# A hybrid attention and convolution layer on one core: norm rows, rotary tables and cached keys loaded by SyncE behind the first modulation's weights, and ten idle products fewer at the start

## The chip, the core and the metric

The kernel runs on one core of a Trainium2 chip, in one launch. The metric is the device time of an execution in microseconds (us); lower is better. Of the engines, PE is TensorE (matmuls; its weight loads are listed apart as PEld), DVE is VectorE, ACT is ScalarE, POOL is GpSimd and SP is SyncE, which here only issues DMA transfers. A transfer can be issued by SP, ACT or POOL.

## What is computed

One layer of a diffusion backbone for 128 context tokens and 512 latent tokens (model width 1024). The reference, cut to what matters:

```python
mod = (silu(cond) @ w_ada + b_ada)                   # shift, scale, gate, twice
h = rms(x, norm_mix) * (1 + sc1) + sh1
q, k, v, gb, gc, u = split(h @ w_in)
q, k = rms(q, q_norm), rms(k, k_norm)                # per head of 64
attn = softmax(rope(q) @ [cache_k, rope(k)].T / 8) @ [cache_v, v]    # latent tokens
y_conv = gb * conv3(gc * u)
x = x + g1 * (concat(rms(attn), rms(y_conv)) @ w_out)
h2 = rms(x, norm_ffn) * (1 + sc2) + sh2
x = x + g2 * ((silu(gate) * up) @ w_down)            # gate, up = split(h2 @ w_gate_up)
```

Context tokens attend to context tokens alone and have no rotary positions. Outputs are the new x of both kinds of token and the context's new keys and values. The cache holds 128 keys and values; `rope` is a table of cosines and sines that is passed in.

## The kernel before, in words

Everything is float32; a product with full precision is made of three matmuls (`mm3`, lines 178 to 181) of a rounded high part and a low part of each operand. Weights come from memory in tiles of 512 KB (128 x 1024), ACT rounds them to a high part `wh`, DVE subtracts to get the low part `wl`.

The change lies in the first stage, some 60 us long, which makes the modulated input h and the query projection. Its steps are written out by hand:

- `P1SEQ` (line 33) is the order of the steps. The recorder goes through it once and each step puts its instructions on its engines, and on PE, DVE, ACT and POOL they stay in that order. The steps that matter here: `dN` is N idle products of the identity with itself (`spin`, line 502, one matmul each, which appears as two records in the trace); `rT` squares token tile T on ACT (line 445), `iT` adds up parts of the square on DVE (459), `kT` sums it on PE (466) and takes the power -1/2 on POOL (189), `oT` spreads it over a row (471, 472). `aK` multiplies the conditioning with the K-th part of the modulation's weights on PE (`ada1_mm`, line 383, sixteen matmuls in two halves of eight, one for each load); `bK` copies the result out, `mK` turns and adds it (427, 429) and makes the scale and shift `modA` and `modB` (399, 400). `gKT`, `hK` and `fKT`, `nK` make the high and low part of h (480, 481, 484), `qKT` is the query projection. `yI`, `zI` split the two halves of the first query weight (531, 535), `w`, `l` split the later weights (522, 539). `p0` is `rows2_load` (lines 544 to 551), `R` builds the rotary tables on DVE (560).
- `LOADS` (line 113) is the order in which SP issues the transfers of this stage: `x` a tile of tokens, `A` the two loads (`af`, 512 KB each) of the next part of the modulation's weights, `Q` and `V` the halves of the first query weight, `W` the next weight of the plan (the query weights 1 to 3, then two for keys and values, then convolution), `C` the cached keys and values (`y`, 64 KB each).

SP works through this list in order, and each issue waits until its buffer is free: there are four `af` buffers, so that the loads of `a2` are issued when PE has done `a0`, and so on, and three buffers (`wf`) for the other weights. Behind a waiting issue all others wait.

`rows2_load` stands in `P1SEQ` between the fourth and fifth part of the modulation. There POOL issues three loads: the norm rows of queries and of keys (64 numbers each, sent to all 128 partitions, 32 KB written) and the rotary tables (256 KB); then it makes four small copies that swap the halves of the norm rows. The rows and tables are read for the first time by step `R`. The cached keys are copied by ACT and the values are split at the start of the attention part, which follows; its instructions are ordered by a scheduler.

Of the kernel before, what the change touches and what calls it, by code (L numbers as in the profile page):

```python
# [15 lines left out]
P = 128  # L16
D = 1024
KD = D // P
NL = 4
# [3 lines left out]
HD = 64  # L23
# [6 lines left out]
NKEY = 640  # L30
EPS = 1e-6
CG = 32
P1SEQ = ('d20 r0 i0h d1 r1 i1e v0 d3 k0 d3 k1 d2 r2 d1 i2e r3 d1 i3f d1 o0 y0 k2 a0 b0 o1 k3 z0 d2 m0 o2 d2 o3 d1 g00 '
# [76 lines left out]
AHEAD = 3  # L110
OSQ = 2
AFB = 4
LOADS = 'xxxxAQAxVAAWCAAAWAWWWWW'
O_Q, O_K, O_GB, O_GC, O_U = 0, 512, 768, 1280, 1792


def build(ctx, tc, x_tiles, cond, cache_k, cache_v, vectors, b_ada, q_norm, k_norm, w_mod, w_ada,
          w_q, w_kv, w_conv, w_out, w_gate_up, w_down, rope, x_turned, o_turned, o_k, o_v):
    nc = tc.nc
    act, dve, pool, pe, sp = nc.scalar, nc.vector, nc.gpsimd, nc.tensor, nc.sync  # L120
# [23 lines left out]
    def T(tag, shape, dt=F32, bufs=1):  # L144
        seq[0] += 1
        return pools[where.get(tag, "A")][1].tile(list(shape), dt, tag=tag, bufs=bufs, name=f"{tag}_{seq[0]}")
# [46 lines left out]
    g = tc.tile_pool(name="R", bufs=1, space=bass.MemoryType.DRAM)  # L193
# [59 lines left out]
    def load_next(later=False):  # L253
        load(order[stream_at[0]], later)
        stream_at[0] += 1
# [81 lines left out]
    def x_load():  # L337
        t = next(xs)
        sp.dma_start(xT[:, t], x_tiles[t])

    def ada1_next(n):
        for _ in range(n):
            next(loads, None)
# [4 lines left out]
                                            mybir.EngineType.SP})  # L348
    pre_order.__enter__()
    first = []  # L350
    for a in LOADS:
        if a == "A":
            ada1_next(3)
        elif a == "W":
            load_next(True)
        elif a == "Q":
            first.append(T("wf", (P, 2, 512), F32, WFB))
            sp.dma_start(first[0][:, 0], order[0][1][:, 0])
            stream_at[0] += 1
        elif a == "V":  # L360
            sp.dma_start(first[0][:, 1], order[0][1][:, 1])
        elif a == "C":
            cc = T("y", (P, 2, NKV, HD))
            ck, cv = cc[:, 0], cc[:, 1]
            sp.dma_start(ck, cache_k[0, 0])
            sp.dma_start(cv, cache_v[0, 0])
        else:
            x_load()
# [18 lines left out]
    def vec_do():  # L387
        for i, (bo, no) in enumerate(((8, V_MIX), (32, V_FFN))):
            dve.scalar_tensor_tensor(nb[:, i], vec[:, bo:bo + KD], 1.0, vec[:, no:no + KD], ALU.add, ALU.mult)
# [148 lines left out]
        wf, wh, wl = rounded.pop(0)  # L538
        eng.tensor_tensor(wl, wf, f32(wh), ALU.subtract)

    gain_rows = {nm: T("gn" + nm, (P, 2, HD)) for nm in "qk"}
    rt = T("oz", (P, 2, NL, HD))

    def rows2_load():
        for nm, g in (("q", q_norm), ("k", k_norm)):
            pool.dma_start(gain_rows[nm][:, 0], g[0].partition_broadcast(P))
        pool.dma_start(rt, rope)
        for nm in "qk":
            g0, g1 = (gain_rows[nm][:, i].rearrange("p (a b c) -> p a b c", a=2, b=2) for i in range(2))
            for b in range(2):  # L550
                pool.tensor_copy(g1[:, :, b], g0[:, :, 1 - b])
# [15 lines left out]
    def q_evict(t):  # L567
# [3 lines left out]
        else:  # L571
            act.activation(qraw[t], qps[t], AF.Copy)

    steps = {"r": x_square, "k": x_rms, "o": x_row, "y": first_hi, "c": late_consts, "w": w_hi, "p": lambda i: rows2_load(),
             "v": lambda i: vec_do(), "m": ada1_mod, "a": ada1_mm, "d": spin, "E": q_evict,
             "R": lambda i: rope_tables(),
             "X": lambda i: act.activation(warm, warm, AF.Exp)}
# [2 lines left out]
    in_pre[0] = True  # L580
    for x in P1SEQ.split():
        k = int(x[1:] if x[0] == "d" else x.strip("p")[1:2] or 0)
# [70 lines left out]
    def k_turn(kd, kt):  # L653
        tag = KTAG[kt]
        tp = PS2()[:, 0, :NKV * P].rearrange("p (v q) -> p v q", v=NKV) if tag == "s" else PB((P, NKV, P), tag=tag)
        for v in range(NKV):
            pe.transpose(tp[:, v], kd[:, v].rearrange("p a d -> p (a d)"), ident)
        ks = slice(kt * P, (kt + 1) * P)
        split(KA[:, :, ks], KB[:, :, ks], tp)
# [4 lines left out]
    def kv_mm(t):  # L664
        acc = PB((P, 256), tag="c")
        s = slice(t * P, (t + 1) * P)
        for k in range(KD):
            wh, wl = W(("kv", k // 4))
            mm3(acc, hH[k][:, s], hL[k][:, s], wh[:, k % 4], wl[:, k % 4], k == 0, k == KD - 1)
        kd = head_norm(acc[:, 0:P], NKV, t, 1)  # L670
        vt = T("vt", (P, NKV, HD), F32, 2)
        act.activation(vt, acc[:, P:].rearrange("p (h d) -> p h d", d=HD), AF.Copy)
        v_store(vt, 0 if t == CTX else t + 2)
        if t == CTX:
            sp.dma_start(o_k[0, 0], kd[:, :, 0])
            sp.dma_start(o_v[0, 0], vt)
        return kd

    def q_split(t):
        return head_norm(qraw[t], NH, t, 0)  # L680

    def q_turn(st, t):
        q = T("qT", (P, NH, P), F32R, QTB)
        tp = PB((P, 4, P)) if t not in QS else PS2()[:, 0].rearrange("p (g q) -> p g q", g=4)
        for g in range(4):
            pe.transpose(tp[:, g], st[:, 2 * g:2 * g + 2].rearrange("p a d -> p (a d)"), ident)
        pairs = q.rearrange("p (g a) q -> p g a q", a=2)
        top, low = slice(0, HD), slice(HD, P)
        with early(QTP):
            for a, x, y in ((0, top, low), (1, low, top)):  # L690
                act.activation(pairs[x, :, a], tp[x], AF.Copy)
                dve.tensor_tensor(pairs[y, :, a], tp[x], f32(pairs[x, :, a]), ALU.subtract)
        return q
# [326 lines left out]
    def k_first():  # L1020
        ks["c"] = k_twice(1)
        act.activation(ks["c"], ck.unsqueeze(2).to_broadcast([P, NKV, 2, HD]), AF.Copy)
        v_store(cv, 1)

    def rms_of(t):
        if t == CTX or t >= 0:
            att_rms(t)

    steps = {"k": lambda t: ks.update({t: kv_mm(t)}), "K": lambda t: k_turn(ks.pop(t), 0 if t == CTX else t + 2),
             "q": lambda t: qs.update({t: q_split(t)}), "Q": lambda t: qT.__setitem__(t, q_turn(qs.pop(t), t)),  # L1030
             "F": F, "A": lambda i: next(ada_gen, None), "c": lambda t: k_first(), "C": lambda t: k_turn(ks.pop("c"), 1),
             "a": ctx_s, "t": ctx_t, "o": ctx_o, "r": att_rms, "M": mix_att}
    for x in SEQ.split():
        if "." in x:
            n, i = (int(y) for y in x[1:].split("."))
# [105 lines left out]
    r2, r2p = {}, {}  # L1141
# [361 lines left out]


tile_hymba = with_exitstack(build)

_INS = ["x_tiles", "cond", "cache_k", "cache_v", "vectors", "b_ada", "q_norm", "k_norm", "w_mod", "w_ada",
# [70 lines left out]
```

## Time and profile before

| | us |
|---|---|
| median of 3 runs | 718.66 (714.97, 718.66, 719.32) |
| the profiled execution | 715.23 |
| its span | 713.5 |
| PE busy | 704.2 |
| DVE busy | 547.4 |
| ACT busy | 418.6 |
| POOL busy | 66.6 |

The span runs from the first to the last instruction of the profiled execution; the rest of its 715.23 us lies around it. A row of the profile's timeline gives the start and the length in us, the engine, the line of the code, what is written and read, how many records, and in brackets how long the engine stood idle before and what ended that. A row of the DMA issues gives what is moved, the engine that issues, how many times, KB of one, and the median of us from the issue to the landing. A row of the stretches gives for each engine the us that it was busy in the stretch and the number of records that start in it, then the granted clock of TensorE, the mean busy share of the 16 DMA engines, and GB/s.

### The profile page before, as it was taken

To read this page: it belongs to the slowest core of one execution; us is meant where nothing else is said; L and a number is where in the kernel's file an instruction comes from. 1 tells how busy PE (TensorE), PEld (TensorE's weight loads), DVE (VectorE), ACT (ScalarE), POOL (GpSimd) and SP (SyncE) were. 2 spreads that over 40 slices of the span, in tenths; PEclk is the share of its full clock that TensorE was granted. 3 is DMA by queue.
4 is the path that set the end of the run, shared out by engine and by line. 5 is a ranking of instruction groups with operands and counts; after the bars stand their busy time and mean duration, and the time that the engine had idled before them with its cause. 6 is when DMAs were issued, how large, how long until landed. Compare 5 with 4: busy or idle time off the path is not lost.

```text
span 713.5 us, 12614 instructions
## 1 busy us (share of the span) xinstructions
PE 704.2 (99%) x4935; PEld 677.7 (95%) x4935; DVE 547.4 (77%) x994; ACT 418.6 (59%) x798; POOL 66.6 (9%) x95
## 2 busy tenths in 40 slices
PE   9899999999999999999999999999999999999998
PEld 8579879988999999999999999999999999999997
DVE  4789979776777746789898966679889756788895
ACT  5456767766677535666565655455556545465553
POOL 2203111112010221300000011000000011000000
PEclk9999999999999999999999999999999999999999
DMA  9957385246322223811222257512222566312462
GB/s 344 342 215 257 119 300 209 72 157 159 154 57 74 61 80 92 278 65 60 90 89 90 89 131 154 127 60 93 85 89 89 126 135 134 110 60 83 140 214 97
DMA packets 34027, 95.95 MB, mean 134 GB/s; under 512 B 4304, under 2 KB 12624, under 8 KB 31920
## 3 DMA queue, kind: packets, MB, share of 16 engines
q1 hardware_dynamic: 29504, 88.09, 35.9%
q0 software_dynamic: 4176, 7.01, 6.9%
q8 instruction: 38, 0.62, 0.3%
q14 instruction: 21, 0.17, 0.1%
q10 hardware_dynamic: 288, 0.05, 0.0%
HBM read 81.77 MB, written 10.62 MB: 129 GB/s over the span
## 4 chain that ended last, share of the span: by engine, by line
PE 96%; DMA 2%; ACT 1%; DVE 0%; issue 0%; POOL 0%; DVEq 0%; POOLq 0%
PE pf L179 22%; PE pf L180 22%; PE pf L181 22%; PE pc L711 4%; PE pc L712 4%; PE pc L713 4%; PE ps L837 2%; PE po L881 2%; PE pt L864 2%; PE pc L768 2%; PE pc L502 2%; DMA af<-in_w_mod_dram 1%; PE ps L179 1%; PE pc L383 1%; PE ps L181 1%; PE ps L180 1%
## 5 line engine op out<-in xcount | busy, mean ns | idle before, releaser
L1348 DVE TENSOR_TENSOR wl<-sx,wh 128x1024 fp32r<-128x1024 f32 (+1 forms) x64 | 75.9, 1186 | 45.9 <-ACT wh L1345 45.9
L179 PE MATMUL pf<-B,wh 128*128 128x320 f32 x288 | 89.1, 309 | 0.0
L180 PE MATMUL pf<-B,wh 128*128 128x320 f32 x288 | 88.9, 309 | 0.0
L181 PE MATMUL pf<-B,wl 128*128 128x320 f32 x288 | 88.9, 309 | 0.0
L181 PE MATMUL pf<-T,wl 128*128 128x320 f32 x280 | 86.6, 309 | 0.0
L180 PE MATMUL pf<-T,wh 128*128 128x320 f32 x280 | 86.5, 309 | 0.0
L179 PE MATMUL pf<-T,wh 128*128 128x320 f32 x280 | 86.5, 309 | 0.0
L1345 ACT ACTIVATE wh<-sx 128x1024 fp32r<-128x1024 f32 (+1 forms) x64 | 65.7, 1027 | 3.8 <-PE pf L180 3.3
L711 PE MATMUL pc<-hH,wh 128*128 128x320 f32 x192 | 61.2, 319 | 0.0
L713 PE MATMUL pc<-hH,wl 128*128 128x320 f32 x192 | 59.3, 309 | 0.0
L712 PE MATMUL pc<-hL,wh 128*128 128x320 f32 x192 | 59.3, 309 | 0.0
L180 PEld LDWEIGHTS pf<-B,wh 128*128 128x128 f32 x288 | 54.1, 188 | 0.0
L179 PEld LDWEIGHTS pf<-B,wh 128*128 128x128 f32 x288 | 54.1, 188 | 0.0
L181 PEld LDWEIGHTS pf<-B,wl 128*128 128x128 f32 x288 | 54.1, 188 | 0.0
L181 PEld LDWEIGHTS pf<-T,wl 128*128 128x128 f32 x280 | 52.6, 188 | 0.1
L179 PEld LDWEIGHTS pf<-T,wh 128*128 128x128 f32 x280 | 52.6, 188 | 0.0
L180 PEld LDWEIGHTS pf<-T,wh 128*128 128x128 f32 x280 | 52.6, 188 | 0.0
L180 PE MATMUL pf<-gT,wh 128*128 128x320 f32 x160 | 49.4, 308 | 0.0
L179 PE MATMUL pf<-gT,wh 128*128 128x320 f32 x160 | 49.4, 308 | 0.0
L181 PE MATMUL pf<-gT,wl 128*128 128x320 f32 x160 | 49.4, 308 | 0.0
L1345 ACT ACTIVATE wh<-wf 128x1024 fp32r<-128x1024 f32 (+3 forms) x48 | 42.6, 887 | 0.8 <-PE pf L180 0.8
L1348 DVE TENSOR_TENSOR wl<-wf,wh 128x1024 fp32r<-128x1024 f32 (+1 forms) x32 | 38.0, 1186 | 4.1 <-ACT wh L1345 4.1
(351 smaller groups left out, 1994.7 us busy)
## 6 DMA issues: line engine op xcount, KB each, us to landing
wf<-in_w_gate_up_dram SPq DMA_DIRECT2D x44, 512.0 KB, 3.3
aw<-in_w_ada_dram SPq DMA_DIRECT2D x10, 1024.0 KB, 5.7
af<-in_w_mod_dram SPq DMA_DIRECT2D x16, 512.0 KB, 7.2
wf<-in_w_down_dram SPq DMA_DIRECT2D x16, 512.0 KB, 3.5
wf<-in_w_conv_dram SPq DMA_DIRECT2D x12, 512.0 KB, 4.2
xd<-cu POOLq DMA_DIRECT2D x16, 320.0 KB, 4.3
mA<-in_w_ada_dram SPq DMA_DIRECT2D x4, 1024.0 KB, 8.5
wf<-in_w_out_dram SPq DMA_DIRECT2D x8, 512.0 KB, 3.5
```

Of the source, the lines that this page charges most:

```text
L179: pe.matmul(out, lh, rh, start=start, stop=False, skip_group_check=more)
L180: pe.matmul(out, lh, rl, start=False, stop=False, skip_group_check=more)
L181: pe.matmul(out, ll, rh, start=False, stop=stop, skip_group_check=more)
L502: pe.matmul(qacc[0][:, :P], ident, ident, start=True, stop=True)
L711: pe.matmul(acc, wh[:, k], hH[k][:, c0:c0 + n], start=(k == 0), stop=False)
L712: pe.matmul(acc, wh[:, k], hL[k][:, c0:c0 + n], start=False, stop=False)
L713: pe.matmul(acc, wl[:, k], hH[k][:, c0:c0 + n], start=False, stop=(k == KD - 1))
L768: pe.matmul(rp[CG * g:CG * (g + 1)], cp[:, k], w[:, g], start=(k == 0), stop=(k == KD - 1), skip_group_check=True)
L837: pe.matmul(s2[:, g, :320], q, kk[:, v, P + g * 320:P + (g + 1) * 320], start=(i == 0), stop=(i == 1))
L864: pe.transpose(tp[:, i, h], u[3][h][:, kt * P:(kt + 1) * P], ident)
L1345: act.activation(wt[x, name][0], src, AF.Copy)
L1348: dve.tensor_tensor(wl, src, f32(wh), ALU.subtract)
```

## The change

Three things are changed. The first group of idle products has 10 in place of 20. The three loads of `rows2_load` are issued by SP, in a new entry `P` of `LOADS`; the swapping copies stay on POOL and at their place in `P1SEQ`. And in `LOADS` the cache loads `C` go from behind the second query weight to behind the fourth, with `P` after them: all modulation and query weights are issued before, the weights of keys and values after.

```diff
-P1SEQ = ('d20 r0 i0h d1 r1 i1e v0 d3 k0 d3 k1 d2 r2 d1 i2e r3 d1 i3f d1 o0 y0 k2 a0 b0 o1 k3 z0 d2 m0 o2 d2 o3 d1 g00 '
+P1SEQ = ('d10 r0 i0h d1 r1 i1e v0 d3 k0 d3 k1 d2 r2 d1 i2e r3 d1 i3f d1 o0 y0 k2 a0 b0 o1 k3 z0 d2 m0 o2 d2 o3 d1 g00 '
-LOADS = 'xxxxAQAxVAAWCAAAWAWWWWW'
+LOADS = 'xxxxAQAxVAAWAAAWAWCPWWWW'
+    gain_rows = {nm: T("gn" + nm, (P, 2, HD)) for nm in "qk"}
+    rt = T("oz", (P, 2, NL, HD))
     for a in LOADS:
...
+        elif a == "P":
+            for nm, g in (("q", q_norm), ("k", k_norm)):
+                sp.dma_start(gain_rows[nm][:, 0], g[0].partition_broadcast(P))
+            sp.dma_start(rt, rope)
         elif a == "C":
...
-    def rows2_load():
-        for nm, g in (("q", q_norm), ("k", k_norm)):
-            pool.dma_start(gain_rows[nm][:, 0], g[0].partition_broadcast(P))
-        pool.dma_start(rt, rope)
+    def rows2_swap():
         for nm in "qk":
             g0, g1 = (gain_rows[nm][:, i].rearrange("p (a b c) -> p a b c", a=2, b=2) for i in range(2))
             for b in range(2):
                 pool.tensor_copy(g1[:, :, b], g0[:, :, 1 - b])
```

PE's start, up to the first spread row: `pc` is the sum that the idle products write, `sq` the squares of a token tile. Before:

```order
L502 MATMUL pc_185<-ident_80 128x128 x24
L466 MATMUL pt_224<-ones_152,sq_211 128x1 x4
L502 MATMUL pc_185<-ident_80 128x128 x3
L466 MATMUL pt_236<-ones_152,sq_215 128x1 x2
L502 MATMUL pc_185<-ident_80 128x128 x5
```

And now:

```order
L508 MATMUL pc_191<-ident_80 128x128 x14
L472 MATMUL pt_217<-ones_158,sq_204 128x1 x4
L508 MATMUL pc_191<-ident_80 128x128 x3
L472 MATMUL pt_229<-ones_158,sq_208 128x1 x2
L508 MATMUL pc_191<-ident_80 128x128 x5
```

The first group (20 + 1 + 3 of `P1SEQ`) has 14 products in place of 24; the rest of PE's order is as it was.

SP's queue around the second query weight, before (`y` holds the cached keys and values, `af` the weights of the modulation):

```order
L226 DMA wf_119<-in_w_q_dram 128x1024
L365 DMA y_121<-in_cache_k_dram 128x128
L366 DMA y_121<-in_cache_v_dram 128x128
L318 DMA af_124<-in_w_mod_dram 128x1024
L318 DMA af_126<-in_w_mod_dram 128x1024
```

And SP's queue from the last query weight on, as it is now (`gnq` and `gnk` are the norm rows, `oz` the rotary tables):

```order
L226 DMA wf_142<-in_w_q_dram 128x1024
L371 DMA y_144<-in_cache_k_dram 128x128
L372 DMA y_144<-in_cache_v_dram 128x128
L366 DMA gnq_95<-in_q_norm_dram 128x64
L366 DMA gnk_96<-in_k_norm_dram 128x64
L367 DMA oz_97<-in_rope_dram 128x512
L226 DMA wf_150<-in_w_kv_dram 128x1024
L226 DMA wf_152<-in_w_kv_dram 128x1024
```

The two cache loads have gone from the first place to the second, and the three loads that POOL issued stand behind them. Before, the two key and value weights followed the last query weight directly.

POOL around these loads, before (`rs` and `rq` are powers of sums of squares):

```order
L189 TENSOR_TENSOR rs_383<-ms_381,neghalf_154 128x1
L546 DMA gnq_186<-in_q_norm_dram 128x64
L546 DMA gnk_187<-in_k_norm_dram 128x64
L547 DMA oz_188<-in_rope_dram 128x512
L551 COPY gnq_186<-gnq_186 128x2x16 x2
L551 COPY gnk_187<-gnk_187 128x2x16 x2
L189 TENSOR_TENSOR rq_728<-ms_726,neghalf_154 128x8
```

Only the three loads are gone from it. On ACT one instruction has moved, the copy of the cached keys: from between the steps of h in front of the second query weight's rounding to behind the rounding of the fourth. DVE's order is as it was.

More of the change, by code (lines that the diff above doesn't have):

```diff
@@ L539, in w_lo @@
         eng.tensor_tensor(wl, wf, f32(wh), ALU.subtract)
-    gain_rows = {nm: T("gn" + nm, (P, 2, HD)) for nm in "qk"}
-    rt = T("oz", (P, 2, NL, HD))
-    def rows2_load():
-        for nm, g in (("q", q_norm), ("k", k_norm)):
-            pool.dma_start(gain_rows[nm][:, 0], g[0].partition_broadcast(P))
-        pool.dma_start(rt, rope)
+    def rows2_swap():
         for nm in "qk":
@@ L572, in q_evict @@
             act.activation(qraw[t], qps[t], AF.Copy)
-    steps = {"r": x_square, "k": x_rms, "o": x_row, "y": first_hi, "c": late_consts, "w": w_hi, "p": lambda i: rows2_load(),
+    steps = {"r": x_square, "k": x_rms, "o": x_row, "y": first_hi, "c": late_consts, "w": w_hi, "p": lambda i: rows2_swap(),
              "v": lambda i: vec_do(), "m": ada1_mod, "a": ada1_mm, "d": spin, "E": q_evict,
```

## The prediction

> **What bounds the kernel now.** I read the page first, then the list of who waited for whom on TensorE, the chain of waits from 20 to 45 us, and the timelines and DMA issues of the first 60 us.
>
> ```profile
> span 713.5 us, 12614 instructions
> PE 704.2 (99%) x4935; PEld 677.7 (95%) x4935; DVE 547.4 (77%) x994; ACT 418.6 (59%) x798; POOL 66.6 (9%) x95
> ...
> PE pc L383 <- DMA af<-in_w_mod_dram: 3.4, 2, 2.2
> PE pc L502 <- POOL ident masks.py:199: 1.6, 1, 1.6
> ```
>
> TensorE is busy 704.2 of 713.5 us, so time can only come from PE work that is dropped, or from its idle 9.3 us. In the list of PE's waits one row matters: 3.4 us, in two waits, for weights of the modulation (af). The chain and PE's timeline show where:
>
> ```profile
> 24.62 9.90 DMA af<-in_w_mod_dram
> ...
> 30.12 0.40 PE L181 MATMUL ps<-wh,hL 128*128 128x512 f32 x1
> 31.69 0.64 PE L383 MATMUL pc<-af,cp 128*32 128x256 f32 x8 [1.17 <-DMA af<-in_w_mod_dram]
> 34.57 0.64 PE L383 MATMUL pc<-af,cp 128*32 128x256 f32 x8 [2.24 <-DMA af<-in_w_mod_dram]
> ```
>
> Step a5 of the hand-written order (ada1_mm(5)) has two halves; the first waits 1.17 us, the second 2.24. The second one's load took 9.90 us to land. Beside it stood GpSimd's three loads. (The last four rows are stretches of 2 us: busy time and count of PE, its weight loads, DVE, ACT and POOL, then granted clock, busy share of the DMA engines, GB/s.)
>
> ```profile
> 24.19 0.80 SPq L318 DMA_DIRECT2D af<-in_w_mod_dram  x2
> ...
> 22.83 0.76 POOL L546 DMA_DIRECT2D gnq<-in_q_norm_dram  x1
> 23.58 0.58 POOL L546 DMA_DIRECT2D gnk<-in_k_norm_dram  x1
> 24.15 0.55 POOL L547 DMA_DIRECT2D oz<-in_rope_dram  x1
> ...
> oz<-in_rope_dram POOLq DMA_DIRECT2D x1, 256.0 KB, 7.7
> gnq<-in_q_norm_dram POOLq DMA_DIRECT2D x1, 32.0 KB, 5.2
> gnk<-in_k_norm_dram POOLq DMA_DIRECT2D x1, 32.0 KB, 6.2
> ...
> 24.00:26.00 2.00, 2.00 (x20) 1.35 (x13) 1.96 (x9) 1.87 (x5) 0.70 (x2) 1.00 1.04 350
> 26.00:28.00 2.00, 2.00 (x16) 1.29 (x18) 2.00 (x4) 1.35 (x3) 0.00 (x0) 1.00 0.99 111
> 28.00:30.00 2.00, 2.00 (x23) 1.34 (x16) 1.73 (x6) 0.00 (x0) 0.88 (x3) 1.00 0.85 344
> 30.00:32.00 2.00, 0.83 (x11) 0.26 (x9) 1.74 (x5) 1.31 (x3) 0.77 (x2) 1.00 1.03 418
> ```
>
> The norm rows land at 22.83 + 5.2 = 28.0 and 23.58 + 6.2 = 29.8, the tables at 24.15 + 7.7 = 31.9. While the rows are under way (26 to 28) the DMA engines are 0.99 busy and yet move 111 GB/s, against 418 when only weights move: the two loads of 32 KB block them. Against 418 that is (1 - 111/418) x 2 = 1.47 us lost there, and (68 + 74)/418 x 2 = 0.68 us in the stretches beside it; the 320 KB themselves are 0.8 us. So the three loads hold up the weights behind them by about 2.9 us, and the a5 waits sum to 3.4.
>
> **The idle products.** The 24 products before step k0 (24 matmuls, two records each) fill 1.58 to 9.09 us:
>
> ```profile
> 1.58 7.51 PE L502 MATMUL pc<-ident 128*128 128x128 f32 x48 [1.58 <-POOL ident masks.py:199]
> 8.93 0.95 PE L466 MATMUL pt<-ones,sq 128*128 128x1 f32 x8
> ...
> 1.50:5.50 4.00, 3.92 (x18) 3.92 (x19) 1.00 0.88 301
> 5.50:8.90 3.40, 3.40 (x32) 3.40 (x30) 1.00 1.02 417
> ```
>
> The mean would price ten products at 20 x 7.51/48 = 3.1 us. But the two lower rows, stretches with line 502's records alone, show 18 of them in the first 4.0 us and then 32 in 3.4: they come twice as fast after 5.5 us. The removed ones are the last of the row, so they cost 20 x 3.40/32 = 2.1 us. I take 2.1. Fourteen products remain, so the switch of pace still falls inside them. What k0 waits for is the square of token tile 0, halved by DVE:
>
> ```profile
> 5.97 0.69 DVE L459 TENSOR_TENSOR sq<-sq 128x512 f32<-128x512 f32 x1 [0.41 <-ACT sq L445]
> 9.91 2.22 ACT L445 ACTIVATE sq<-xT 128x1024 f32<-128x1024 f32 x2 [2.88 <-PE pt L466]
> ```
>
> It is ready at 5.97 + 0.69 = 6.66; PE would come at 8.93 - 2.1 = 6.8. Nothing is lost, and ACT's next squares, which today wait 2.88 us for k0 to free their buffer, follow 2.1 us earlier. Next late is the first query weight:
>
> ```profile
> wf<-in_w_q_dram SPq DMA_DIRECT2D x1, 256.0 KB, 7.2
> 12.54 0.62 ACT L531 ACTIVATE wh<-wf 128x512 fp32r<-128x512 f32 x1
> 14.46 0.69 DVE L535 TENSOR_TENSOR wl<-wf,wh 128x512 fp32r<-128x512 f32 x1
> 15.15 0.17 DVE L429 TENSOR_REDUCE modt<-pt 128x4 f32<-128x16 f32 x1
> ```
>
> That row is the load issued at 4.76, so it lands at 4.76 + 7.2 = 11.96; ACT rounds it until 11.96 + 0.62 = 12.58, and DVE's subtraction, which stands ahead of the first modulation (modt), can't start before. It starts at 14.46 now: 14.46 - 12.58 = 1.9 us are left of the 2.1. After that PE wants weights that are still coming in:
>
> ```profile
> af<-in_w_mod_dram SPq DMA_DIRECT2D x1, 512.0 KB, 6.0
> 20.56 1.07 PE L383 MATMUL pc<-af,cp 128*32 128x256 f32 x16
> ```
>
> This is the second load for step a2, issued at 14.03 when a0 freed its buffer, landed at 14.03 + 6.0 = 20.0. PE needs it half way through a2, at 20.56 + 0.5 = 21.1; in the new order at 19.2. Its issue moves 1.9 us forward too, but the engines were full (share 1.02 up to 8.90, above), so it may land less early: 18.1 if it keeps its latency, 20.0 if the queue in front of it is all that counts. The loss lies between 0 and 0.8 us; I take 0.3, nearer the first, since the loads land 512 KB in 1.25 us at 418 GB/s and two of them behind the query weight of 7.26 + 9.3 (next row) end at 19.1.
>
> ```profile
> wf<-in_w_q_dram SPq DMA_DIRECT2D x1, 256.0 KB, 9.3
> ```
>
> Head: 1.9 - 0.3 = **1.6 us**.
>
> **The moved loads.** With the rows, the tables and the two cache loads gone from in front, the a5 loads come 1.25 us apart behind those of a4. Today they are issued at 24.19 and 24.62; the new PE frees their buffers some 1.6 us earlier, at 22.6 and 23.0. An undisturbed load of this size just ahead took 5.4 to 6.2 us from issue to landing:
>
> ```profile
> af<-in_w_mod_dram SPq DMA_DIRECT2D x1, 512.0 KB, 5.4
> af<-in_w_mod_dram SPq DMA_DIRECT2D x1, 512.0 KB, 6.2
> ```
>
> So they land near 28.0 and 29.2. PE wants them at 30.12 + 0.40 - 1.6 = 28.9 and half a us later. Both waits go: **3.4 us**. If the queue keeps 1 us more than this, 0.8 of it comes back as a wait; if it keeps none, nothing more is won. What follows a5 has a cover. ACT's rounding of the third query weight waits for its load today:
>
> ```profile
> 38.31 1.06 ACT L522 ACTIVATE wh<-wf 128x1024 fp32r<-128x1024 f32 x1 [6.53 <-DMA wf<-in_w_q_dram]
> 38.40 0.18 DVE L429 TENSOR_REDUCE modt<-pt 128x4 f32<-128x16 f32 x1 [0.97 <-PE pt L427]
> ```
>
> ACT idles 6.53 us there, yet PE loses nothing after 35.2; and DVE, which has run on while PE stood, is still waiting for PE (0.97 us) at 38.40, so it has room to follow a PE that does not stand. That load stands three places behind the a5 ones, so it moves forward with them (29.2 + 3 x 1.25 = 33.0, that is 5.3 us earlier). The last two modulation loads (a6, a7) stand beside it and have the same lead.
>
> Now the five loads' new place: SyncE's queue, after the last query weight, ahead of the kv weights.
>
> ```profile
> 36.12 0.42 SPq L226 DMA_DIRECT2D wf<-in_w_kv_dram  x1
> wf<-in_w_kv_dram SPq DMA_DIRECT2D x1, 512.0 KB, 7.8
> 50.85 0.75 DVE L560 TENSOR_TENSOR tab<-oz,gnq 128x256 f32<-128x256 f32 x2
> 51.98 2.94 ACT L522 ACTIVATE wh<-wf 128x1024 fp32r<-128x1024 f32 x3
> ```
>
> SyncE issues the first kv weight at 36.12 today, some 5 us earlier in the new order, less the five issues ahead of it (5 x 0.42 = 2.1 us). The slow stretch of the rows, some 2 us, goes with them to the weights behind. The kv weight lands at 36.12 + 7.8 = 43.9 and ACT takes it at 51.98; five us less on both sides, and 4.1 more on the load, leave 4 us of cover. The tables, landing near 31 + 2.1 + 7.7 = 41, are read by DVE at 50.85 - 5 = 45.8. GpSimd's four swapping copies wait for the rows, and behind them it has nothing until the first heads' norms. ACT's copy of the cached keys moves with its load, behind the rounding of the last query weight, which comes in just before it. I cost all this at nothing; without the cover it would be at most the 4.1 us.
>
> **Sum.** 1.6 + 3.4 = **5.0 us**. The profiled execution took 715.23 us (713.5 span and 1.7 around it), so the same execution would take 710.2. The three timed runs of before lie at 714.97, 718.66 and 719.32, so 5.0 less is 713.7 on their median. Where in that scatter new runs will lie I can't tell, and predict the middle, 712.0 us.
>
> **Rivals.**
> - The stream of weights bounds the head. PE comes earlier but a1 to a3 wait for their loads, which need the bytes ahead of them to pass. For it: share 1.02. Against: loads are issued on PE's release of a buffer, and that moves too. Then the head gives 0.8 or less (the upper end of the loss above, and more) and the sum is near 4 us: 711.2 on the profiled execution's scale. 18%.
> - The rows hold a5 by their bytes alone, and the slow stretch has another cause that stays. Then the a5 waits shrink by the 0.8 us of 320 KB at 418 GB/s, and 1.6 + 0.8 = 2.4 us are won: 712.8. Against it stands the stretch at 111 GB/s, which begins when the rows go out and ends when they have landed. 8%. The Trainium skill, DMA: Bandwidth & Descriptors, "Anatomy of one DMA", takes this side: a DMA costs 2.0 us of latency and its bytes at 436 GB/s, by which the three would fill the engines for an estimated 0.75 us, where the rows above give 2.9.
> - More than I count: the head keeps its 2.1, and the cache loads' 128 KB (0.3 us at 418 GB/s) count too: 5.8 us or more, 709.4. 9%.
> - Slower: the idle products are what keeps TensorE at its fast pace. If the pace falls back after k0, where waits are now closer, each us of PE work from 6.8 on costs 2. It decides from 5 us of such work on; up to a2 there are 20.56 - 8.93 = 11.6 us of it, and the time would be 715.2 - 5.0 + 11.6 = 721.8. Against it: in the old trace PE stood still for 2.24 us inside a5, and the eight records behind that gap took the same 0.64 us as the eight before it, with the granted clock at 1.00 in every window. 5%. The Trainium skill, TensorE: Matmul & The Clock Gate, "What's actually happening", is the rule behind this rival: the clock doubles after a busy window of about 3.4 us, halves after an idle one, and the windows' phase varies from run to run. The trace agrees with the first (twice the pace after some 4 us of products); an idle stretch of that length it doesn't have.
>
> **How the numbers follow.** 60% for the forecast, the rivals as given. A measurement of this kernel tells about 1% (7.2 us) from no change. The forecast of 5.0 us is 0.7%, so "within 1%" holds most of it and of the first two rivals; the scatter of 4.4 us between runs of one kernel carries some over the bound: 0.20 faster, 0.74 within, 0.06 slower. The range starts a little under the third rival (709.4) and ends with the second (712.8) on the level of the median of before (plus 3.4), rounded up: 708.5 to 716.5. The last rival is left outside.
>
> **What would show it.** Right: PE's record x28 in place of x48 at 1.58, k0 near 6.8 without idle time; no row "PE pc L383 <- DMA af" over 1 us in PE's waits; SyncE issuing five small loads after the last query weight; DVE's table products without a wait. Wrong: a wait of PE at L383 before 25 us (first rival), one at a5 near 29 us that is still 2 us or more (second), records of 0.2 us spacing after k0 (the last), or a DVE or ACT wait for oz, gnq, y or the kv weight.

## The result, and the profile after

Eleven runs of each kernel: a median of 717.38 us before (714.66 to 719.99) and 713.30 after (712.24 to 715.33). The ratio is estimated at 0.9946, with a 95% interval of 0.9927 to 0.9965: 0.54%, or 3.9 us, faster. That is within 1%, and inside the range. The two profiled executions are closer together, 715.23 and 712.77 us, and what makes the difference between 2.5 and 3.9 is the main finding below.

The head of the page after, and from the list of what PE waited for the rows that are new or longer (us in total, times, the longest):

```profile
span 711.0 us, 12574 instructions
PE 703.1 (99%) x4915; PEld 676.2 (95%) x4915; DVE 547.3 (77%) x994; ACT 418.6 (59%) x798; POOL 64.9 (9%) x92
```

```profile
PE pc L389 <- ACT res L424: 0.6, 1, 0.6
PE ps L838 <- ACT pr L848: 0.6, 2, 0.3
...
PE pc L389 <- DMA af<-in_w_mod_dram: 0.4, 1, 0.4
PE pc L179 <- DVE of L571: 0.3, 1, 0.3
```

The 3.4 us for the modulation's weights have become 0.4; 0.6 us for a copy of ACT and 0.3 for one of DVE are new, and the wait of line 838, in the attention part, has grown from 0.2 us to 0.6. The timeline of PE shows the places (line 389 was 383, line 508 was 502):

```profile
1.57 6.22 PE L508 MATMUL pc<-ident 128*128 128x128 f32 x28 [1.57 <-POOL ident masks.py:199]
7.63 0.95 PE L472 MATMUL pt<-ones,sq 128*128 128x1 f32 x8
...
20.30 0.64 PE L389 MATMUL pc<-af,cp 128*32 128x256 f32 x8 [0.39 <-DMA af<-in_w_mod_dram]
...
29.73 1.07 PE L389 MATMUL pc<-af,cp 128*32 128x256 f32 x16
...
37.39 1.07 PE L389 MATMUL pc<-af,cp 128*32 128x256 f32 x16 [0.63 <-ACT res L424]
```

x28 stands in place of x48, and a5, at 29.73, is one piece of sixteen matmuls without a gap. Before, it was two pieces with 1.17 and 2.24 us ahead of them.

Set side by side step for step, the new PE is ahead of the old by 1.3 us at k0 (8.93 against 7.63), 0.7 after a2, 4.4 after a5, 3.7 after a7, 3.4 after the first kv product, and 2.5 at the end.

The chain of waits shows why a2 waits, and what brings about the wait at a7 (start, length):

```profile
12.74 7.51 DMA af<-in_w_mod_dram
20.30 0.64 PE pc L389 x8
...
28.52 6.57 DMA wf<-in_w_q_dram
35.13 0.94 issue
36.07 1.00 ACT hH L487 x2
37.07 0.27 ACT res L424
37.39 1.07 PE pc L389 x16
```

The second load of a2 lands at 12.74 + 7.51 = 20.25. The third query weight lands at 35.09. ACT rounds it first, and the copy of a6's result, whose buffer a7 needs, stands behind that rounding on ACT.

Last, the moved loads and their readers, from the timelines of SP, DVE and ACT:

```profile
34.10 0.45 SPq L366 DMA_DIRECT2D gnq<-in_q_norm_dram  x1
34.59 0.43 SPq L366 DMA_DIRECT2D gnk<-in_k_norm_dram  x1
35.10 0.39 SPq L367 DMA_DIRECT2D oz<-in_rope_dram  x1
36.42 2.67 SPq L226 DMA_DIRECT2D wf<-in_w_kv_dram  x2
```

```profile
47.56 0.75 DVE L561 TENSOR_TENSOR tab<-oz,gnq 128x256 f32<-128x256 f32 x2
```

```profile
40.98 0.40 ACT L1023 ACTIVATE mA<-y 128x256 f32<-128x256 f32 x1
```

The tables land at 35.10 + 6.1 = 41.2 and DVE reads them at 47.56; neither this row nor that of the cached keys has a bracket for idle time. POOL alone stands: its swapping copies wait 17.29 and 0.84 us for the rows, and behind them it has nothing to do until 57.4 us.

### The profile page after: what moved, and what is told of

The parts are those of the page before. It is cut to its first block, busy times and chain, and to the rows that moved or that the text cites. A ratio compares the mean times of both kernels' runs of the same rounds, so it can differ in the third digit from the quotient of the medians.

```text
span 711.0 us, 12574 instructions
## 1 busy us (share of the span) xinstructions
PE 703.1 (99%) x4915; PEld 676.2 (95%) x4915; DVE 547.3 (77%) x994; ACT 418.6 (59%) x798; POOL 64.9 (9%) x92
## 4 chain that ended last, share of the span: by engine, by line
PE 90%; DMA 3%; DVE 3%; ACT 2%; issue 1%; POOL 0%; DVEq 0%; SPq 0%; POOLq 0%; ACTq 0%
PE pf L179 22%; PE pf L180 22%; PE pf L181 22%; PE pc L712 3%; PE pc L713 3%; PE pc L714 3%; PE po L882 2%; PE pt L865 2%; PE ps L838 2%; PE pc L769 2%; DMA es<-t 1%; PE pc L508 1%; DMA af<-in_w_mod_dram 1%; DMA wf<-in_w_q_dram 1%; PE pc L389 1%
```

## The experiments

Four were run with the kernel before beside them (33 runs, median 717.04), then four (30 runs, 716.83), then four (19 runs, 716.58). Every run also gives its mean granted clock, and that turned out to be needed. Of these 82 runs of the kernel before, 35 (12, 13 and 10) have a clock of 0.999 or 1.0, with medians of 715.2, 715.5 and 715.1 us in the three groups. The other 47 lie between 0.994 and 0.998, with medians of 718.1, 717.6 and 719.2.

### The parts one by one

**spin10_only:** the kernel before with `d10` in place of the first `d20`.

> The kernel before with 10 in place of 20 idle products, and nothing else. Theory A (the parts add up: the products are worth some 2 us at the fast pace, the loads some 3.4): 1.5 to 2.2 us faster, ratio 0.997 to 0.998, the two waits of PE in a5 still there and together about 3 us, since GpSimd's loads move forward with PE. Rival B (the stream of loads bounds the head whatever PE does): PE comes to a5 earlier and waits there longer by as much, 5 us or more, and the time is as before within 0.5 us.

713.77 us, ratio 0.9954 (0.9936 to 0.9972). In its list of PE's waits the a5 stand is smaller, 1.7 and 0.5 us, but there:

```profile
PE pc L383 <- DMA af<-in_w_mod_dram: 2.4, 3, 1.7
...
PE pc L383 <- ACT res L418: 0.5, 1, 0.5
```

11 of its 12 runs have a clock of 0.999 or more. Against the runs of before with such a clock (715.2) it is only 1.5 us faster. So more is won than theory A had, but by the clock, and B is out; the a5 stand came to 2.2 us in place of the 3 that A expected.

**rows_only:** `LOADS = 'xxxxAQAxVAAWCAAAWAWPWWWW'` in the kernel before, rows and tables by SP behind the last query weight; the cache loads and the 20 products as before.

> The kernel before with the norm rows and tables issued by SyncE behind the last query weight; the cache loads and the 20 idle products as before. Theory A: the a5 waits of 3.4 us go, 2.5 to 3.5 us faster, ratio 0.995 to 0.9965. Rival (it is the cache loads that matter, since they stood ahead of a4's and a5's loads): a5 still waits 1 us or more and less than 1 us is won.

713.16 us, 0.9951 (0.9931 to 0.9971), all clocks at 0.999 or more; PE waits 0.3 us for `af`. Theory A holds, and the rival is out.

**cache_only:** `LOADS = 'xxxxAQAxVAAWAAAWAWCWWWW'`, only the cache loads moved.

> The kernel before with only the two cache loads moved behind the last query weight; rows and tables still issued by GpSimd amid the weights. Theory A: the 128 KB are worth 0.3 us at a5, ratio 0.999 to 1.0; a5 still waits 2.5 to 3.5 us. Rival: they are the load that a5 waits for, and more than 1.5 us is won.

717.38 us, 1.0004 (0.9982 to 1.0027), and 10 of 12 clocks under 0.999. Moving the cache loads by themselves is worth nothing that these runs show. In its profile PE stands 2.4 us at a5, where it was 3.4 before; the stand isn't the same in every execution.

The products alone give 3.3 us and the rows alone 3.5; together they give 3.9. They don't add up, so in part they remove the same thing. One part of that is the clock, as shown below. It isn't all: in the runs with a clock of 0.999 or more the products give 1.5 us and the rows 2.1, and both together 1.9 to 2.4.

### Is it GpSimd's way of loading, or the place of the rows?

**rows_sp_amid:** the three loads by SP, but still between the loads of a4 and those of a5, with `d20`.

```diff
-LOADS = 'xxxxAQAxVAAWAAAWAWCPWWWW'
+LOADS = 'xxxxAQAxVAAWCAPAAWAWWWWW'
```

> The kernel before with the three loads issued by SyncE in place of GpSimd, but still amid the modulation's weights, between the loads of a4 and those of a5; 20 idle products, cache loads as before. Theory Q (it is GpSimd's issuing that is slow: its packets hold the engines for 1 to 2 us each, SyncE's take under 0.1): the stretch of low GB/s is gone, a5 waits 0.3 to 1.2 us for the bytes of the three loads, 2.2 to 3.2 us faster than before, ratio 0.9955 to 0.997. Theory P (it is the place: 256 sends of 256 B from one address are slow wherever they run, and only hidden at the end of the queue): a5 waits 3 us or more, same time as before.

716.77 us, 0.9993 (0.9974 to 1.0012): no gain, as theory P has it, though the wait at a5 is 2.2 us and not 3. Its waits and its stretches of 1 us from 26 to 28 (the last three numbers are the granted clock, the share of the DMA engines and GB/s):

```profile
PE pc L389 <- DMA af<-in_w_mod_dram: 2.2, 2, 1.6
```

```profile
26.00:27.00 1.00, 1.00 (x6) 0.68 (x4) 1.00 (x2) 0.87 (x3) 0.00 (x0) 1.00 0.67 213
27.00:28.00 1.00, 1.00 (x18) 0.32 (x16) 1.00 (x2) 0.17 (x1) 0.20 (x1) 1.00 0.27 102
```

The slow stretch comes with the rows on SP's queue too, at 102 GB/s, though here the engines are idle in it (0.27), where GpSimd's loads kept them busy (0.99 before). The packets of 256 bytes in which SP's rows go take 15 to 18 ns each. So it is the place of the rows that counts, and not the engine that issues them. In the changed kernel the stretch is found again where the rows now stand:

```profile
37.00:38.00 1.00, 0.61 (x12) 0.41 (x16) 1.00 (x2) 0.63 (x3) 0.00 (x0) 1.00 0.81 252
38.00:39.00 1.00, 1.00 (x16) 0.57 (x5) 1.00 (x2) 0.00 (x0) 0.00 (x0) 1.00 0.43 147
```

### Why runs of before differ: the clock

The theory formed here was that PE's stand at a5 costs twice: the time that PE stands, and in most runs a stretch of halved clock behind it.

**before_filled:** idle products ahead of both halves of a5 in the kernel before, written to the unused half of its bank, so that PE works where it stood. They stand amid a5's sum in that bank, and this kernel leaves part of a5's modulation out of its result; it serves for its time alone.

```diff
+            for _ in range((5, 9)[h] if k == 5 else 0):
+                pe.matmul(two[:, 256:256 + P], ident, ident, start=True, stop=True, skip_group_check=True)
             for i in range(4):
                 cond_mm(rp, 4 * h + i, wf[:, i].rearrange("p a b -> p (a b)"))
```

> The kernel before with 5 idle products ahead of the first half of a5 and 9 ahead of the second, into an unused part of a5's own bank, so that PE has work in the 3.4 us in which it stands there. Nothing is loaded earlier. Theory C (the stand at a5 lets TensorE's clock fall in some executions, which costs these 1.7 us or 3.4 us more; of the 33 runs of the kernel before, the 13 with a granted clock of 0.999 or 1.0 lie at 714.0 to 716.7 and the 20 with 0.994 to 0.998 at 716.4 to 720.2): all runs have 0.999 or 1.0, the median falls to 715 to 715.5, ratio 0.997 to 0.998. Rival (the low clock comes by chance, whatever PE does): the low clocks stay in about 6 of 10 runs and the ratio is 1.0 or above, since the 14 products may cost up to 0.5 us.

716.21 us, 0.9994 (0.9978 to 1.0009). PE's timeline:

```profile
31.06 1.28 PE L413 MATMUL pc<-ident 128*128 128x128 f32 x10
32.45 0.64 PE L383 MATMUL pc<-af,cp 128*32 128x256 f32 x8
33.02 2.27 PE L413 MATMUL pc<-ident 128*128 128x128 f32 x18
35.22 0.64 PE L383 MATMUL pc<-af,cp 128*32 128x256 f32 x8
```

The median is not the 715 to 715.5 us that was expected; the spread is what counts. All 12 clocks are at 0.999 or 1.0, and the runs lie within 715.15 to 717.25, where the 30 runs of before beside them lie within 713.64 to 720.83, 17 of them under 0.999. The products keep the clock and cost PE about 0.7 us (716.2 against 715.5 at equal clock). (Of the 33 runs that the expectation counts, 12 have the high clock and 21 the low one.)

**a5_later:** `LOADS = 'xxxxAQAxVAAWCAWAAAWWWWW'` in the kernel before: the third query weight is loaded ahead of a5's weights, so that PE stands longer in one piece.

> The kernel before with the third query weight (512 KB) loaded ahead of the weights of a5 instead of behind those of a6, so that PE stands longer at a5, some 4.5 us in place of 3.4. By the stand alone: 1.2 us slower at a5, given back in part because that query weight comes early. Theory C: the clock falls more often or for longer, granted 0.995 or less in most runs, and the trace itself may show a stretch behind a5 with the matmuls at twice their length; median 1.5 to 3.5 us slower than before, ratio 1.002 to 1.005. Rival (clock by chance): 0 to 1.2 us slower with the same spread of clocks.

718.32 us, 1.0024 (1.0003 to 1.0046). All ten runs have a clock of 0.994 to 0.998, and its profile shows what that is (stretches, then PE's timeline):

```profile
32.00:36.00 4.00, 1.73 (x16) 0.43 (x16) 1.01 (x2) 1.67 (x4) 0.86 (x2) 0.68 0.95 388
36.00:40.00 4.00, 4.00 (x22) 2.38 (x20) 2.20 (x7) 1.01 (x2) 0.00 (x0) 0.50 0.95 289
40.00:44.00 4.00, 4.00 (x30) 2.64 (x22) 2.62 (x8) 0.79 (x2) 0.00 (x0) 0.97 0.76 285
```

```profile
30.73 0.39 PE L180 MATMUL ps<-wl,hH 128*128 128x512 f32 x1
...
34.17 2.27 PE L383 MATMUL pc<-af,cp 128*32 128x256 f32 x16 [2.82 <-DMA af<-in_w_mod_dram]
...
37.28 0.63 PE L180 MATMUL ps<-wl,hH 128*128 128x512 f32 x1
```

PE stands 2.82 us, less than the 4.5 that were expected but in one piece, and behind the stand the same matmul takes 0.63 in place of 0.39 us. The clock records have the half clock from 33.43 to 40.26, that is 6.83 us, in which up to 3.4 us of work are lost (PE stood for the first 0.74 of it). These records begin where the full pace does, at 6.13 us here; ahead of that the rows of stretches show 1.00 at half pace too, and a run's mean clock does not count that start.

Two stretches cut at the clock's own steps show when it falls. At full clock the records' lengths are whole multiples of 3.413 us (27.31 us, 8 of them, ahead of the drop here; 706.56, 207 of them, in before), and 6.83 is two of them; so I take the steps as a fixed grid and cut the windows there. In a5_later the window that ended in the drop, and in the kernel before the two that contain the a5 stand:

```profile
30.02:33.43 3.41, 1.33 (x6) 0.75 (x4) 2.76 (x9) 2.10 (x4) 1.21 (x4) 1.00 0.90 350
```

```profile
29.45:32.86 3.41, 1.71 (x13) 0.72 (x11) 2.53 (x7) 1.31 (x3) 0.97 (x2) 1.00 1.03 419
32.86:36.28 3.42, 1.71 (x14) 1.16 (x15) 0.97 (x5) 0.00 (x0) 0.00 (x0) 1.00 1.00 404
```

With 1.33 us of PE work in such a window the clock halved, with 1.71 twice in a row it didn't. The end of the kernel says the same in every one of the 14 profiles: the clock halves once more when PE has no work left, which costs nothing but is why a run without any loss can have 0.999. The fullest window that ended in such a drop is this one of cache_only:

```profile
707.61:711.02 3.41, 1.45 (x10) 1.19 (x9) 1.69 (x4) 0.00 (x0) 0.00 (x0) 1.00 0.36 134
```

Over all 14, at full clock, windows with 1.45 us of work or less were followed by half clock, windows with 1.71 or more were not. Back to full pace it went only behind windows with some 2.9 us of PE work or more, at the start of these profiles as in a5_later; 2.67 us in before_af6 was not enough. So the second window of a5_later, which began in the stand and held 2.57 us, cost another one:

```profile
33.43:36.84 3.41, 2.57 (x19) 0.91 (x19) 0.34 (x1) 0.27 (x1) 0.00 (x0) 0.50 0.92 350
```

In this execution of before the grid cut the stand of 1.17 and 2.24 us in two. Had the window begun at 31.1, it would have held 0.64 us of work. The grid lies differently in each execution (full pace began at 5.56 us in the profile of before, at 7.54 in that of after, and between 4.47 and 7.66 in the others), which is how the same kernel can lose the clock in some runs and keep it in others. That the 47 runs lost it by this count is argued from the one trace in which the loss was caught; no profiled execution of the kernel before itself shows a drop there. Nor does the count give the share of such runs: of all positions that the grid can have over the profile of before, 85% give a window with under 1.45 us of PE work, and 36% over that of cache_only, while 57% of the runs of the one and 10 of 12 of the other lost the clock. The length of the stand differs between executions too. Its sizes fit: one window at half clock costs 3.41/2 = 1.7 us, two cost 3.4, and in the first group the 11 runs of before at 0.997 and 0.998 have a median of 717.3, the 10 at 0.994 to 0.995 of 718.8, against 715.2.

### What is left in the changed kernel

**after_b6dve:** step `b6a` becomes `b6`, so DVE in place of ACT makes the copy that a7 waits for.

> The changed kernel with the copy of a6's result made by DVE in place of ACT, where it stands behind the rounding of the late third query weight. The wait of 0.6 us at a7 (PE for ACT res) goes; if it is only that, 0.3 to 0.6 us faster than the changed kernel, 712.8, ratio to before 0.9938 to 0.9945. Rival (the weights behind it bound the head anyway): the wait turns up at a later place and the time is that of the changed kernel, ratio 0.9946.

713.34 us, 0.9960 (0.9945 to 0.9975). The a7 wait is gone from the list, and the time isn't better. As the rival has it, the wait turns up later: PE is 4.1 us ahead of before at the first kv product, where the changed kernel is 3.4 ahead, but its wait at line 838 is then 0.8 us, and at 177 us the lead is down to 2.3.

**after_af6:** the same with `AFB = 6`, six buffers for the modulation's weights in place of four.

> The same with six buffers for the modulation's weights in place of four, so that the loads are issued one part further ahead of PE. Theory A (what is left in the head is the stream of loads that waits for PE to free a buffer): the loads of a2 to a6 come closer together, the third query weight lands 1 us earlier or more, PE has no wait for af, and 0.8 to 1.5 us are won over the changed kernel, ratio to before 0.992 to 0.9935. Rival (the stream is bound by its bytes at 412 GB/s all the way): no earlier landing, same time as the changed kernel.

712.16 us, 0.9941 (0.9920 to 0.9963), without any wait for `af` in its profile: 1.2 us under after_b6dve, from which it differs by the buffers alone.

### The last four: an early issue in place of another order

**before_af6:** the kernel before with one number changed.

```diff
-AFB = 4
+AFB = 6
```

> The kernel before with six buffers for the modulation's weights in place of four; GpSimd's loads, the cache loads and the 20 idle products stay where they were. The loads of a5 then wait for a2 instead of a3 and go out some 3 us earlier, ahead of GpSimd's three loads. Theory (what costs time is PE's stand at a5, by itself and by the half-rate clock that it sets off, wherever the load's lateness comes from): the wait for af at a5 goes, all runs are at a granted clock of 0.999 or more, and the median is 3 to 4 us under that of the kernel before, as if the loads had been moved. Rival (GpSimd's loads hold up whatever is under way beside them, so that an earlier issue only moves the wait to the next load, a6 or a query weight): the wait for af or for wh stays at 1.5 us or more, and the gain is 1.5 us or less.

712.73 us, 0.9938 (0.9911 to 0.9964), all clocks at 1.0. PE's list of waits has no row for `af` any more, and a5 is one piece:

```profile
31.46 1.07 PE L383 MATMUL pc<-af,cp 128*32 128x256 f32 x16
```

GpSimd's loads still stand amid the weights and still hold up the second half of a5 (its first half lands at 28.23, the second at 30.56), but now 0.9 us before a5 starts. a5's two loads are issued at 22.26 and 22.69, in front of GpSimd's, where they were issued at 24.19 and 24.62, behind them. So the place of the rows had mattered only because a5's loads came after them. The rival falls.

**after_again**, the changed kernel as it is, and **after_af6_again**, the kernel of after_af6 once more:

> The changed kernel once more, as it is, beside the two that follow. Both theories: 3.9 us less than the kernel before, within its interval of 2.5 to 5.2; all runs at a granted clock of 0.999 or more.

> The changed kernel with six buffers for the modulation's weights and the copy of step b6 on DVE, once more, for a direct comparison with the changed kernel on the same chip. Theory (0.4 + 0.6 us of waits for weights and for the copy are left in the changed kernel, and six buffers remove them): about 1 us under the changed kernel. Rival (the 1.1 us between the two medians of different calls is scatter): no difference over 0.4 us.

713.40 us, 0.9956 (0.9932 to 0.9981), and 711.86 us, 0.9924 (0.9897 to 0.9951). Six buffers, with the copy on DVE, are 1.5 us better here and 1.1 against the first measurement. In runs of equal clock (712.83 against 711.86) it is 1.0. The two intervals overlap, but both carry the scatter of the kernel before; set against each other, all six runs (up to 712.16) lie under all nine (from 712.25), so that scatter alone is unlikely.

**af6_d20:** the same with `d20` again.

> The same with 20 idle products in the first group again. Theory (with loads early enough the head is bound by PE, and the ten products are worth their 2.2 us at the fast pace): 1.5 to 2.2 us over the kernel of the run before. Rival (the stream of weights bounds the head in any case): the same time within 0.5 us, with waits of PE for af or wh in one that are not in the other.

712.98 us, 0.9941 (0.9920 to 0.9962): the ten products are worth 1.1 us here (0.8 against after_af6, the same kernel), half of their 2.2 or less. Where the other half goes stands in PE's timelines, of af6_d20 first, which has no stand at a2, then of after_af6_again and after_again:

```profile
20.09 1.24 PE L389 MATMUL pc<-af,cp 128*32 128x256 f32 x16
```

```profile
20.09 0.64 PE L389 MATMUL pc<-af,cp 128*32 128x256 f32 x8 [1.10 <-DMA af<-in_w_mod_dram]
```

```profile
20.39 0.64 PE L389 MATMUL pc<-af,cp 128*32 128x256 f32 x8 [0.98 <-DMA af<-in_w_mod_dram]
```

The second load of a2, from issue to landing in us, and the landing of the first one:

| kernel | issued | landed | first load landed |
|---|---|---|---|
| before | 14.03 | 20.0 | 18.7 |
| after | 12.74 | 20.25 | 17.8 |
| after_again | 12.24 | 20.34 | 17.7 |
| after_af6_again | 9.59 | 20.04 | 17.3 |
| af6_d20 | 9.95 | 20.65 | 17.8 |
| before_af6 | 9.89 | 20.18 | 19.1 |

4.4 us of earlier issue move the landing by nothing, and PE meets it at 20.0 to 20.7 however early it comes. The bytes in front do not explain that. The half query weight ahead of these loads lands at 16.0 to 16.6, and the first load 1.2 to 1.3 us behind it in four of these kernels, as 512 KB at 418 GB/s would; by the same count the second would land at 18.5 to 19.1. In these four it lands 2.5 to 2.8 us behind the first, and in before_af6 the first is late already (2.8 us behind that query weight). What holds them up was not tried.

## Why the prediction was right, and where it was not

**The time** came out in the range, 713.3 against 712.0, by errors of opposite sign, which is luck: too much for the head and nothing for what is given back behind a5, and on the other side nothing at all for the clock.

**Idle products, 2.1 us: right in size, but not all of it is won.** Ten cost 2.2 us at the fast pace. In the two profiled executions only 1.3 showed at k0, since the pace of after rose 2.0 us later (the stretches of after):

```profile
5.50:7.50 2.00, 2.00 (x12) 2.00 (x11) 1.15 (x4) 1.75 (x2) 0.00 (x0) 1.00 1.03 420
7.50:8.90 1.40, 1.40 (x14) 1.40 (x14) 1.24 (x5) 0.28 (x1) 0.04 (x1) 1.00 1.03 421
```

12 records in 2.0 us, then 14 in 1.4: the step that I saw at 5.5 us stands at 7.5 here. So my k0 of 6.8 was a number of one execution.

**Head, loss of 0.3 at a2: mis-sized, the first step that failed.** I took a value "nearer the first" of two bounds, with a landing near 19.1. The landing did not move at all (table above), so the upper end, 20.0, was the right one, and an execution in which the pace rises early stands longer than my bound of 0.8: 0.98 and 1.10 us. The second half of a2 began at 21.0 before and can begin at 20.0 to 20.7 now, so the head is worth 0.3 to 1.0 us, 0.7 in the profiled pair, not 1.6. The first rival, the stream of weights, had this size right (0.8 or less) but is not shown by it: the first load of a2 came by the bytes in front, in time, and the second 1.2 to 1.6 us later than these would have it, for a cause that stays open.

**Moved loads, 3.4 us: right.** a5's loads land at 27.79 and 29.03 (I said 28.0 and 29.2), and PE, coming at 29.73, doesn't stand. That the landings fit so well is luck: they were issued 0.9 us later than I said (23.49 and 23.92) and took 4.3 and 5.1 us in place of 5.4 and 6.2. What I put down to GpSimd's queue is a matter of place: by SP at the same place the rows hold up a5 just as well. And with the a5 loads issued 1.9 us earlier the rows do no harm where they were.

**"The slow stretch of the rows, some 2 us, goes with them": right.** It is found at 37 to 39 us, with 147 GB/s in its second half, and is covered as I said. Neither PE, DVE nor ACT waits for rows, tables, kv weights or cached keys.

**What follows a5 has a cover: wrong by 1.9 us, the larger error.** PE's lead falls from 4.4 after a5 to 2.5 at the end. The third query weight was to land at 33.0 and landed at 35.09, since its issue, at 28.52, stood behind those of a6's loads, which waited for PE to free their buffers (from 28 to 29 us the DMA engines moved 86 GB/s), and ACT's copy for a7 stood behind its rounding. But mending that (after_b6dve) gains nothing, so the lead is then given back elsewhere. 0.3 us of it is the wait for DVE's copy of line 571 and some 0.4 the longer wait of line 838 for ACT at 92 us; where the last tenths go is left open.

**Not in the sum at all: the clock.** At equal clock the change is worth 715.2 - 712.8 to 713.3, that is 1.9 to 2.4 us, about what the profiled pair shows (2.5). The rest of the 3.9 comes from runs: 47 of 82 of the kernel before lost one or two windows, a mean of 0.57 x 2.6 = 1.5 us (2.6 us lie between the mean of these runs and that of the others); of the 20 runs of the changed kernel 18 lost none, and what took the clock in the other two, at 0.998, no profile shows. I had given a falling clock 5%, as a danger to the new kernel, and argued from the old trace that a stand of 2.24 us does it no harm. It was one execution, of the sort in which nothing happened. The mechanism was there, in the kernel before.

**The rivals.** The first is spoken of above. The second is excluded: the waits for `af` at a5 did not shrink by 0.8 us but ended (rows_only), and the stretch went along with the rows. The third needed 5.8 us, which were not there. The last did not happen: in the profile after, the clock stays at 1.0 from 7.5 us until PE's last work is done. The Trainium skill, TensorE: Matmul & The Clock Gate, "What's actually happening", which I weighed there, speaks of an idle window of about 3.4 us. By the windows above a mostly idle one is enough: the clock halved after one that held 1.33 us of PE work, and after one that held 1.45.

## What to carry to other kernels

Before valuing a stall of the engine that bounds a kernel, sort the runs of that kernel by their granted clock: a stand of 2 to 3 us can cost another 1.7 or 3.4 us in those executions where it fills most of a window, and a profile from an execution that got away shows none of it. When a load is late, ask first whether it was issued late, since two more buffers did here what a new order of loads and queues did. And before counting on work removed ahead of a load, look whether the landing follows the issue; where it doesn't, as at a2 here, the engine only comes earlier to the same wait.

## What the runs showed of the hardware that was not expected

- The clock of TensorE is at 1.0 or at 0.5 in windows of 3.41 us that don't start with the work: full pace began between 4.47 and 7.66 us in the profiles of kernels whose first product stands at 1.57 to 1.58. It halved after windows with 1.45 us of PE work or less, and came back after windows with some 2.9 us or more.
- Rows of 256 bytes to each of 128 partitions slow the loads around them to 100 to 150 GB/s from either queue: with busy engines from GpSimd's (0.99), with idle ones from SP's (0.27 and 0.43). It was milder in the kernels with six buffers, where the rows' packets go out among those of the weights in front (258 GB/s from 35 to 36 us in after_af6_again).
- In ten of the 14 profiles a packet of 16 KB on the queue for instructions, which took 0.96 to 1.11 us, began between 16.9 and 18.0 us. In eight of them a2's second load lands 1.8 to 2.8 us behind the first; in the other two (before_af6, cache_only), and in the four profiles where that packet came earlier or later, 1.1 to 1.3 us behind. That the packet is the cause was not tried.
